# A hybrid encoder on one core: attention's first loads inside the projections, the short sequence's sums on DVE, and a group's last value products in front of its sums over keys

## Chip, core and metric

One core of one Trainium2 chip runs the whole layer. The metric is the device time in microseconds (us); three runs of the kernel before were timed, and one more execution was profiled. The engines are named as the profile names them: PE is TensorE (PEld its weight loads), DVE is VectorE, ACT is ScalarE, POOL is GpSimd, SP is SyncE, which issues nearly all transfers (SPq is its queue).

## The reference

One encoder layer on two requests that share weights: a prompt of 1024 tokens and a sample of 2048, 1024 channels, each with 256 memory tokens. All numbers are fp32.

```python
h = rms_norm(x, norm_pre)
z = einsum('btd,de->bte', h, w_in)          # 2304 columns
u_pool, g_pool, q, k, v, g_attn, q_x, g_x = split(z, SPLITS)
pool_out = multiscale_pool(u_pool, pool_w, pool_scale) * silu(g_pool)   # windows 2, 4, 8, 16
q, k = apply_rope(rms_norm(q)), apply_rope(rms_norm(k))                 # 8 heads, 2 key/value heads, 64 wide
attn_out = softmax(q k^T / 8) v * silu(g_attn)                          # every query sees every key
x_out = softmax(q_x k_m^T / 8) v_m * silu(g_x)                          # 4 heads, 256 memory tokens
mix = concatenate([pool_out, attn_out, x_out])                          # 1024 columns
return x + rms_norm(einsum('bte,ed->btd', mix, w_out), norm_post)
```

## The kernel before

Matrix products keep fp32 accuracy by splitting each operand in a high part (type fp32r) and a rest: three matmuls, hi·hi, lo·hi and hi·lo, stand for one. The kernel has two phases, each with its own pools of SBUF and PSUM, and the second phase's pools open when the first one's have closed.

**Projections** (lines 72 to 427). Four super-blocks run one after the other: the memory tokens, the prompt, and the two halves of the sample. A token super-block has 1024 tokens in two blocks of 512 and walks over six groups of 384 columns of w_in (`tok_groups`): queries (`group_n0`), memory queries and gates (`ct[2]`), keys, values and the last queries (`group_n1`), pooling input and its first gate (`ct[0]`), gates (`ct[1]`), and memory query and gates (`ct[3]`). In a transposed group every `product` makes a 128×512 tile in PSUM (`pz`, four buffers) with 24 matmuls, eight channel chunks of three. Results go to scratch in DRAM through SP's queue: `dq`, `dqx` (queries), `dk`, `dkm` (keys), `dv`, `dvm` (values), `dg` (gates, after Silu), `dp` (pooled channels). The pooling mixer (`pool_chunk`) adds shifted copies on POOL in the buffers `s2`, `s4`, `sm`, multiplies on PE (`pm`), scales on DVE into `s4` and stores that to `dp`; the next chunk writes `s4` again.

**Attention** (lines 430 to 878). Work is cut into pairs of query tiles (256 queries): eight of the sample, then four of the prompt. A pair has three groups, one for each of the two key/value heads and one for the memory (kinds 0, 1, 2). A group has 16 chunks of 128 keys in the sample, 8 in the prompt and 2 in the memory; one chunk of one group is a slot, 344 in all. A hand-written order holds for PE, ACT, DVE and POOL. In a slot stand:

- `weights(k, 0)` and `weights(k, 1)`: scores S of 128 keys by 512 queries on PE (L595; L599 for the memory), from KA and qa, and from KB and qb; then exp on ACT into P (L602), six buffers.
- `sums(k-1)`: z, the running sum of P over chunks (L613), 1024 columns, cut by `CUT = 512`: the first 512 on POOL, the others on DVE.
- one `largest`, a "look": two matmuls (L567) or four (L559) make 1024 scores N in PSUM (pool `psn`, two buffers), and DVE reduces them (L570) to a row maximum. A group's looks run LEAD = 4 slots and more before the group. The twenty looks that the first groups need come ahead of slot 0.
- `values`, in runs of four chunks: acc, P times V (L625).
- at a group's end `totals` (L633: z times ones, over the partitions, into a buffer of `psn`), `take` (acc times gate), `inverse` (rz, which is written to DRAM as `rows` and read back as `gz`, spread over partitions), and `mix_out`: o times gz on POOL (L661), the cast to the high part of mix on ACT and the rest on POOL (both L784).
- pieces of an earlier pair's output product (L726 to L728), eight of three matmuls for each half of a token tile, until slot HOLD = 16 or 26 of the next pair; then squares on ACT, y on DVE (L752), the residual xr + y on POOL (L755) and the store.

The queries' and keys' first loads (`load`), and V, gates, w_out and norm_post (`load_late`, `load_w_out`, `load_npost`) go through SP's queue. The last pair's output stays in PSUM (`both`) and its two tiles take turns on one buffer each of xr and y.

What places a group's last value products and its totals, with n the group's first slot and c its chunks:

```python
            for k in range(0, c, RUN):
                ks = list(range(k, min(k + RUN, c)))
                at(n + ks[-1] + 1 + END, g.values, ks)
            at(n + c + 1 + END, g.totals)
```

Of the kernel before, what the change touches and what calls it, by code (L numbers as in the profile page):

```python
# [15 lines left out]
D = 1024  # L16
# [7 lines left out]
def encoder(ctx, tc, I, O):  # L24
# [46 lines left out]

    with ExitStack() as p1:
# [3 lines left out]
        pst = p1.enter_context(tc.tile_pool(name="pst", bufs=2, space=PSUM))  # L76
# [15 lines left out]
        def hT_block(sb, blk):  # L92
# [4 lines left out]
            for i in range(4):  # L97
                x = two.tile([128, D], F32, name="x", tag="x", bufs=4)
                nc.sync.dma_start(out=x, in_=rows(sb, blk, i))
                if kind not in gains:  # L100
                    gains[kind] = one.tile([128, D], F32, name="gain", tag="gain")
                    src = I["mem_norm" if kind == "mem" else "norm_pre"]
                    nc.sync.dma_start(out=gains[kind], in_=src.broadcast_to([128, D]))
                junk = one.tile([128, D], mybir.dt.bfloat16, name="junk", tag="junk")
                ss = two.tile([128, 1], F32, name="ss", tag="ss")
                nc.scalar.activation(out=junk, in_=x, func=AF.Square, accum_out=ss)
                r = rsqrt(two, ss, 1, D, "rsx")
# [27 lines left out]
        def product(ps, terms):  # L135

            n = len(terms)
            for c, (sh, sl, mh, ml) in enumerate(terms):
                nc.tensor.matmul(ps, lhsT=sh, rhs=mh, start=c == 0, stop=False)  # L139
                nc.tensor.matmul(ps, lhsT=sh, rhs=ml, start=False, stop=False)  # L140
                nc.tensor.matmul(ps, lhsT=sl, rhs=mh, start=False, stop=c == n - 1)  # L141

# [9 lines left out]
        def transposed(hT, w, col):  # L152
# [3 lines left out]
            product(ps, [(w[0][:, c, f], w[1][:, c, f], hT[0][:, c], hT[1][:, c]) for c in range(NC)])  # L156
# [5 lines left out]
        def rope_tables():  # L162
            out = []
            raw = [two.tile([128, NTT, 64], F32, name="ropec", tag="ropec", bufs=1),
                   two.tile([128, NTT, 64], F32, name="ropes", tag="ropes", bufs=1)]
            for r, key in zip(raw, ("rope_c", "rope_s")):
                nc.sync.dma_start(out=r, in_=I[key])
            for key in ("k_norm", "q_norm"):
                g = one.tile([128, 2, 64], F32, name="hg", tag="hg" + key)
# [9 lines left out]
                for j in range(2):  # L179
                    if key == "q_norm":  # L180
                        t = raw[j]
                    else:
                        t = one.tile([128, NTT, 64], F32, name="ropek", tag=f"ropek{j}")
# [7 lines left out]
        def norm_rope(ps, parts, tt):  # L191
# [3 lines left out]
            z = two.tile([128, 384], F32, name="z", tag="z")  # L195
            sq = two.tile([128, 384], F32, name="sq", tag="sq")
            t1 = two.tile([128, 384], F32, name="t1", tag="t1")
            nc.scalar.copy(out=z[:, 0:w], in_=ps[:, 0:w])
            nc.scalar.activation(out=sq[:, 0:w], in_=ps[:, 0:w], func=AF.Square)
            ss = two.tile([128, 6], F32, name="ssh", tag="ssh")  # L200
# [3 lines left out]
            r = rsqrt(two, ss[:, 0:n], n, 64, f"rsh{n}")  # L204
# [22 lines left out]
        def heads_transposed(src, npair):  # L227
# [4 lines left out]
            o = two.tile([128, 2, 3, 128], F32R, name="qst", tag="qst")  # L232
# [20 lines left out]
        def group_n1(s, b, hT, w):  # L253
            for i in range(4):
                tt = 4 * b + i
                ps = natural(hT, w, i, 0, 384)
                vst = two.tile([128, 2, 64], F32, name="vst", tag="vst")
# [104 lines left out]
        def chunks_group(chunks):  # L362
            def run(s, b, hT, w):
                for k, (_, f, args) in enumerate(chunks):
                    f(s, b, *args, transposed(hT, w, 128 * k))
# [25 lines left out]
        def mem_v(s, b, hT, w):  # L391
            for i in range(4):
                ps = natural(hT, w, i, 0, 256).rearrange("p (h d) -> p h d", d=64)
                vst = two.tile([128, 4, 64], F32, name="vmst", tag="vmst", bufs=1)
# [15 lines left out]

        for sb, (kind, s, nb, b0) in enumerate(SB):
            groups = groups_of(sb)
            nxt = []
            for gi, (src, pieces, run) in enumerate(groups):
# [5 lines left out]
                final = gi + 1 == len(groups)  # L420
                for blk in range(nb):
                    if kind == "mem" and gi == 0 and blk == 0:
                        nxt.append(hT_block(sb + 1, 0))
                    run(s, b0 + blk, cur[blk], w)
# [5 lines left out]
    with ExitStack() as p2:  # L430
        def pool(name, bufs, space=bass.MemoryType.SB):
            return p2.enter_context(tc.tile_pool(name=name, bufs=bufs, space=space, reuse_waits="tile"))

        one = pool("p2one", 1)
        two = pool("p2two", 2)
        pss = pool("pss", 2, PSUM)
        psn = pool("psn", 2, PSUM)
        psa = pool("psa", 1, PSUM)
        pso = pool("pso", 1, PSUM)

        ones = one.tile([128, 32], F32, name="ones")
        nc.vector.memset(ones, 1.0)

        KA = [one.tile([128, 2048], F32R, name=f"KA{kind}") for kind in range(2)]
        KB = [one.tile([128, 2048], F32R, name=f"KB{kind}") for kind in range(2)]
        KA.append(one.tile([128, 2, 2, NMEM], F32R, name="KA2"))
        KB.append(one.tile([128, 2, 2, NMEM], F32R, name="KB2"))
        for t in KB:  # L450
            nc.vector.memset(t[64:65].bitcast(F32), 1.0)
        V = [one.tile([128, 16, 64], F32, name=f"V{kind}") for kind in range(2)]
        V.append(one.tile([128, 2, 4, 64], F32, name="V2"))
        has_K, has_V = set(), set()

        def load_K(s, kind):
            has_K.add((s, kind))
            for hl in range(2):
                for t, h in ((KA, 64 * hl), (KB, 0))[:2 - hl]:
                    if kind == 2:  # L460
                        src = DKM[hl, :, :, s].rearrange("d (c j) m -> d c j m", j=2)
                        nc.sync.dma_start(out=t[2][h:h + 64].bitcast(F32), in_=src)
                        continue
                    for a in range(0, SEQS[s][1], 1024):
                        nc.sync.dma_start(out=t[kind][h:h + 64, a:a + 1024].bitcast(F32),
                                          in_=DK[s][kind][hl, :, a:a + 1024])

        def load_V(s, kind):
            has_V.add((s, kind))
            if kind == 2:  # L470
                nc.sync.dma_start(out=V[2], in_=DVM[s])
                return
            for a in range(0, SEQS[s][1] // 128, 8):
                nc.sync.dma_start(out=V[kind][:, a:a + 8], in_=DV[s][kind][:, a:a + 8])

        wo_hi = one.tile([128, NC, D], F32R, name="wo_hi")
        wo_lo = one.tile([128, NC, D], F32R, name="wo_lo")
        raws = {}

        def load_w_out(c):  # L480
            raws[c] = two.tile([128, D], F32, name="raw", tag=("y", "xr")[c % 2], bufs=1)
            nc.sync.dma_start(out=raws[c], in_=I["w_out"][0, 128 * c:128 * c + 128])

        def split_w_out(c):
            raw = raws.pop(c)
            nc.scalar.copy(out=wo_hi[:, c], in_=raw)
            nc.gpsimd.tensor_tensor(out=wo_lo[:, c], in0=raw, in1=wo_hi[:, c].bitcast(F32), op=ALU.subtract)

        npost = one.tile([128, D], F32, name="npost")

        def load_npost():
            nc.sync.dma_start(out=npost, in_=I["norm_post"].broadcast_to([128, D]))


        lanes32 = {}
        for name in ("top",):
            lanes32[name] = [one.tile([128, 32], F32, name=f"{name}{n}") for n in range(2)]
            for t in lanes32[name]:
                nc.vector.memset(t, 0.0)

        def lanes_to_rows(t, name):

            r = two.tile([128, 32], F32, name="rows32", tag=f"r{name}")
            nc.vector.transpose(out=r, in_=t)
# [416 lines left out]
```

## Time and profile before

| | |
|---|---|
| runs | 1940.56, 1941.95, 1943.42 us; median 1941.95 |
| profiled execution | 1940.45 us; span from first to last instruction 1938.6 us |
| granted TensorE clock | 0.974 mean |
| busy | PE 1830.0 us (94%), DVE 1126.4 (58%), POOL 914.3 (47%), ACT 699.3 (36%) |
| projections end on PE | 691.78 us |
| first exp of attention | 747.73 us |
| first slots of the pairs 9 to 12 (prompt) | 1601.2, 1672.4, 1746.8, 1820.8 us |
| last matmul | 1923.7 us |

Times are microseconds from the first instruction. In a timeline row stand start, duration, engine, line, operation, output and inputs, and in brackets how long the engine had been idle and what ended that. The row of a tile gives minimum, median and maximum of its durations in nanoseconds.

### The profile page before, as it was taken

To read this page: it belongs to the slowest core of one execution; us is meant where nothing else is said; L and a number is where in the kernel's file an instruction comes from. 1 tells how busy PE (TensorE), PEld (TensorE's weight loads), DVE (VectorE), ACT (ScalarE), POOL (GpSimd) and SP (SyncE) were. 2 spreads that over 40 slices of the span, in tenths; PEclk is the share of its full clock that TensorE was granted. 3 is DMA by queue.
4 is the path that set the end of the run, shared out by engine and by line. 5 is a ranking of instruction groups with operands and counts; after the bars stand their busy time and mean duration, and the time that the engine had idled before them with its cause. 6 is when DMAs were issued, how large, how long until landed. Compare 5 with 4: busy or idle time off the path is not lost.

```text
span 1938.6 us, 23683 instructions
## 1 busy us (share of the span) xinstructions
PE 1830.0 (94%) x8520; PEld 1289.7 (67%) x8520; DVE 1126.4 (58%) x1304; ACT 699.3 (36%) x1266; POOL 914.3 (47%) x816
## 2 busy tenths in 40 slices
PE   7999999999999938999999999999999999999995
PEld 6998898978998824456565655656565655565564
DVE  6833254422623018876767677676767666756742
ACT  5522242313422102543434444443434443333331
POOL 3735033620634003863746456373746454635644
PEclk9999999999999967899999999999999999999998
DMA  6653355434443273212112021222212143323211
GB/s 235 200 147 89 110 161 138 116 100 123 118 123 86 66 176 118 82 39 77 60 47 80 26 79 44 77 60 77 61 48 78 49 125 83 93 77 104 82 39 60
DMA packets 148486, 181.84 MB, mean 94 GB/s; under 512 B 21504, under 2 KB 118416, under 8 KB 148368
## 3 DMA queue, kind: packets, MB, share of 16 engines
q1 hardware_dynamic: 148368, 180.33, 32.6%
q8 instruction: 67, 1.10, 0.2%
q14 instruction: 51, 0.42, 0.1%
HBM read 126.50 MB, written 53.62 MB: 93 GB/s over the span
## 4 chain that ended last, share of the span: by engine, by line
PE 70%; issue 10%; DVE 8%; POOL 6%; DMA 4%; ACT 2%; SPq 1%; POOLq 0%; ACTq 0%; DVEq 0%
PE acc L625 13%; PE S L595 11%; PE pz L141 9%; PE pz L139 9%; PE pz L140 9%; PE N L567 6%; PE py L726 3%; PE py L727 3%; PE py L728 3%; DVE nb L570 2%; POOL z L613 2%; DVE z L613 2%; PE S L599 1%; POOL rs L63 1%; PE N L633 1%
## 5 line engine op out<-in xcount | busy, mean ns | idle before, releaser
L602 ACT ACTIVATE P<-S 128x512 f32<-128x512 f32 x688 | 401.3, 599 | 612.8 <-PE S L595 435.4
L613 POOL TENSOR_TENSOR z<-z,P 128x512 f32<-128x512 f32 x272 | 389.2, 1431 | 260.3 <-ACT P L602 253.9
L570 DVE TENSOR_REDUCE nb<-N 128x1 f32<-128x1024 f32 x256 | 311.0, 1218 | 229.0 <-PE N L567 228.2
L625 PE MATMUL acc<-P,V 128*64 128x512 f32 (+1 forms) x1472 | 318.2, 574 | 0.5
L595 PE MATMUL S<-qa,KA 128*128 128x512 f32 x640 | 277.3, 433 | 11.6 <-ACT P L602 11.5
L613 DVE TENSOR_TENSOR z<-z,P 128x512 f32<-128x512 f32 x272 | 262.2, 964 | 15.9 <-ACT P L602 15.4
L567 PE MATMUL N<-KA,qa 128*128 128x512 f32 x640 | 217.0, 423 | 46.1 <-DMA qa<-dq 29.5
L595 PE MATMUL S<-qb,KB 65*128 65x512 f32 x640 | 255.2, 399 | 0.0
L139 PE MATMUL pz<-hT_hi,w_hi 128*128 128x512 f32 x592 | 233.2, 394 | 2.6 <-ACT w_hi L68 1.8
L140 PE MATMUL pz<-hT_lo,w_hi 128*128 128x512 f32 x592 | 233.9, 395 | 0.0
L141 PE MATMUL pz<-hT_hi,w_lo 128*128 128x512 f32 x592 | 232.3, 392 | 0.0
L595 PEld LDWEIGHTS S<-qa,KA 128*128 128x128 f32 x640 | 121.7, 190 | 146.4 <-issue 71.9
L625 PEld LDWEIGHTS acc<-P,V 128*64 128x64 f32 x1472 | 98.1, 137 | 177.6 <-issue 168.5
L567 PEld LDWEIGHTS N<-KA,qa 128*128 128x128 f32 x640 | 119.3, 198 | 97.5 <-DVE nb L570 35.1
L63 POOL TENSOR_TENSOR rs<-rs,mhalf 128x1 f32<-128x1 f32 (+2 forms) x100 | 92.9, 932 | 175.7 <-DVE rs L61 175.5
L570 DVE TENSOR_REDUCE top<-N 128x1 f32<-128x1024 f32 (+1 forms) x88 | 107.1, 1218 | 109.5 <-PE N L567 79.6
L613 POOL TENSOR_TENSOR z<-P 128x512 f32<-128x512 f32 x36 | 46.6, 1294 | 215.4 <-ACT P L602 154.3
L140 PE MATMUL pz<-w_lo,hT_hi 128*128 128x384 f32 (+1 forms) x416 | 140.5, 338 | 0.9 <-DVE w_lo L69 0.8
L141 PE MATMUL pz<-w_hi,hT_lo 128*128 128x384 f32 (+1 forms) x416 | 140.2, 338 | 0.0
L139 PE MATMUL pz<-w_hi,hT_hi 128*128 128x384 f32 (+1 forms) x416 | 139.4, 336 | 0.0
L726 PE MATMUL py<-wo_hi,mix 128*128 128x512 f32 x352 | 138.0, 392 | 0.0
L727 PE MATMUL py<-wo_lo,mix 128*128 128x512 f32 x352 | 137.2, 390 | 0.0
(115 smaller groups left out, 2587.5 us busy)
## 6 DMA issues: line engine op xcount, KB each, us to landing
wraw<-w_in SPq DMA_DIRECT2D x15, 1536.0 KB
dg<-gst SPq DMA_DIRECT2D x48, 256.0 KB
qa<-dq SPq DMA_DIRECT2D x48, 256.0 KB
gz<-rows SPq DMA_DIRECT2D x72, 128.0 KB
x<-x_sample SPq DMA_DIRECT2D x16, 512.0 KB
xr<-x_sample SPq DMA_DIRECT2D x16, 512.0 KB
y_sample<-xr SPq DMA_DIRECT2D x16, 512.0 KB
dq<-qst SPq DMA_DIRECT2D x48, 128.0 KB
```

Of the source, the lines that this page charges most:

```text
L63: nc.gpsimd.tensor_tensor(out=r, in0=r, in1=mhalf[:, 0:n], op=ALU.pow)
L139: nc.tensor.matmul(ps, lhsT=sh, rhs=mh, start=c == 0, stop=False)
L140: nc.tensor.matmul(ps, lhsT=sh, rhs=ml, start=False, stop=False)
L141: nc.tensor.matmul(ps, lhsT=sl, rhs=mh, start=False, stop=c == n - 1)
L567: nc.tensor.matmul(S[:, 512 * b:512 * b + 512], lhsT=q, rhs=KA[self.kind][:, k:k + 512], start=True, stop=True)
L570: nc.vector.tensor_reduce(out=out, in_=S, axis=AX.X, op=ALU.max, negate=True)
L595: nc.tensor.matmul(S, lhsT=K[self.kind][rows_, keys], rhs=q, start=n == 0, stop=n == 1)
L602: nc.scalar.activation(out=self.P[k][:, j], in_=S, func=AF.Exp)
L613: e.tensor_tensor(out=z[:, x], in0=a[:, x], in1=P[:, x], op=ALU.add)
L625: nc.tensor.matmul(self.acc[64 * j:64 * j + 64, x], lhsT=v, rhs=P[:, j, x], start=(k, i) == (0, 0), stop=k == self.chunks - 1, skip_group_ ...
L726: nc.tensor.matmul(ps, lhsT=mh, rhs=wo_hi[:, c, cols], start=first, stop=False)
L727: nc.tensor.matmul(ps, lhsT=mh, rhs=wo_lo[:, c, cols], start=False, stop=False)
```

## The change

The attention's definitions (`Group`, `Pair`, `Output`, the tables of slots and looks) now stand ahead of the projections, and their pools are renamed; that alone moves no instruction. Four things differ.

1. The projections' buffers that only the first three groups of a super-block need are in pools of their own (`front`) which close ahead of the last super-block's fourth group. In their place opens a pool `early` with KA, KB (without KB of kind 1), qa, qb and the looks' results, and the first groups' loads are issued there. The PSUM pool of the transposes (`heads`) closes ahead of the fifth group, and `psn` opens. In the sixth group PE's order is written out, and after every second channel chunk of a product stands one look. KB is loaded when a group's row maxima are turned into rows of qb (`shift`), KA before. KB of kind 1 lives in a pool that opens after the projections, and its row of ones is written there.
2. `CUT` is 0 for the prompt: its sums over keys are one DVE instruction of 1024 columns, and none on POOL.
3. A group's last run of values stands a slot later, directly in front of its totals.
4. The last pair's two output tiles take xr and y from the six buffers of P, and their loads are issued at their first piece.

```diff
+                if last and gi == 3:
+                    front.close()
+                    early = ctx.enter_context(tc.tile_pool(name="early", bufs=1, side="right", reuse_waits="tile"))
+                    open_early()
+                    for g in loads.pop(-1):
+                        g.load()
+                if last and gi == 4:
+                    heads.close()
+                    psn = ctx.enter_context(tc.tile_pool(name="psn", bufs=2, space=PSUM, side="right", reuse_waits="tile"))
...
+                    if last and final:
+                        with tc.manual_schedule(engines={mybir.EngineType.PE}):
+                            run(s, b0 + blk, cur[blk], w, look_ahead)
...
+        def product(ps, terms, beside=lambda: None):
...
                 nc.tensor.matmul(ps, lhsT=sl, rhs=mh, start=False, stop=c == n - 1)
+                if c % 2:
+                    beside()
...
+    def look_ahead():
+        if ahead:
+            g, n = ahead.pop(0)
+            g.largest(n)
...
-        with tc.manual_schedule(engines=order):
-            with tc.high_priority(offset=2000):
-                for g in loads.pop(-1):
-                    g.load()
-                for g, n in ahead:
-                    g.largest(n)
...
         def load(self):
-                if (s, kind) not in has_K:
-                    load_K(s, kind)
+            for hl in range(2):
+                load_K(s, kind, KA, hl, 64 * hl)
...
         def shift(self):
...
+            load_K(self.s, self.kind, KB, 0, 0)
             self.load_q(self.qb[0:64], 1)
...
-        CUT = 512
+    CUT = (0, 512)
...
-                for e, x in ((nc.gpsimd, slice(0, CUT)), (nc.vector, slice(CUT, 1024))):
-                    e.tensor_tensor(out=z[:, x], in0=a[:, x], in1=P[:, x], op=ALU.add)
+            cut = CUT[self.s]
+            if cut:
+                nc.gpsimd.tensor_tensor(out=z[:, :cut], in0=a[:, :cut], in1=P[:, :cut], op=ALU.add)
+            nc.vector.tensor_tensor(out=z[:, cut:], in0=a[:, cut:], in1=P[:, cut:], op=ALU.add)
...
-                at(n + ks[-1] + 1 + END, g.values, ks)
+            at(n + ks[-1] + (2 if ks[-1] == c - 1 else 1) + END, g.values, ks)
...
         def start(self):
-                self.xr = two.tile([128, D], F32, name="xr", tag="xr", bufs=1)
+            tag = dict(tag="P", bufs=6) if self.last else dict(tag="xr", bufs=1)
+            self.xr = dbl.tile([128, D], F32, name="xr", **tag)
...
         def piece(self, h, c, first, final):
             if self.last:
                 if self.both is None:
+                    self.start()
                     self.both = psn.tile([128, 1024], F32, name="N", tag="N")
```

PE at the end of the projections, before (pz is a product's tile, N a look's; KA_5966 and KA_5967 are kinds 0 and 1, KA_5970 the memory):

```order
L139 MATMUL pz<-hT_hi,w_hi 128x512
L140 MATMUL pz<-hT_lo,w_hi 128x512
L141 MATMUL pz<-hT_hi,w_lo 128x512
L567 MATMUL N<-KA_5966,qa 128x512 x28
L559 MATMUL N<-KA_5970,qa 128x256 x8
```

and now, inside a product of the sixth group (KA_5376 is kind 0):

```order
L551 MATMUL pz<-hT_hi,w_lo 128x512
L191 MATMUL N<-KA_5376,qa 128x512 x2
L549 MATMUL pz<-hT_hi,w_hi 128x512
L550 MATMUL pz<-hT_lo,w_hi 128x512
L551 MATMUL pz<-hT_hi,w_lo 128x512
```

The looks stood in one block behind the last product; now one stands after every six matmuls of the sixth group's first five products.

SP's queue behind the projections' key stores, before:

```order
L237 DMA dk_114<-qst 64x2x128
L338 DMA dp_112<-s_5394 128x512
L343 DMA dg_2_0_98<-gst 512x1x128
L338 DMA dp_112<-s_5433 128x512
L343 DMA dg_3_0_107<-gst 512x1x128
```

and now:

```order
L649 DMA dk_114<-qst 64x2x128
L99 DMA KA_5378<-dk_114 64x1024 x4
L161 DMA qa<-dq_0_1_76 64x1024 x2
L96 DMA KA_5379<-dkm 64x4x256 x2
L161 DMA qa<-dqx_0_79 64x1024 x2
L99 DMA KA_5376<-dk_114 64x1024 x4
L161 DMA qa<-dq_0_0_75 64x1024 x2
L750 DMA dp_112<-s_5437 128x512
L755 DMA dg_2_0_98<-gst 512x1x128
```

Sixteen loads of 256 KB stand between the last dk store and the first dp store of that super-block.

PE in the prompt where a group ends (py is an output piece), before:

```order
L727 MATMUL py<-wo_lo,mix 128x512
L728 MATMUL py<-wo_hi,mix 128x512
L633 MATMUL N<-z,ones 32x256 x4
L595 MATMUL S<-qa,KA_5967 128x512
L595 MATMUL S<-qb,KB_5969 128x512
```

and now:

```order
L358 MATMUL py<-wo_lo,mix 128x512
L359 MATMUL py<-wo_hi,mix 128x512
L252 MATMUL acc<-P,V_6121 64x512 x8
L260 MATMUL N<-z,ones 32x256 x4
L220 MATMUL S<-qa,KA_5378 128x512
L220 MATMUL S<-qb,KB_6119 128x512
```

The last eight value products, which stood a slot earlier, now stand directly in front of the totals.

More of the change, by code (lines that the diff above doesn't have):

```diff
@@ new lines, in encoder @@
+    looks, n = {}, len(slots)
+    left = {g: list(range(len(g.pieces))) for g in groups}
+    while any(left.values()):
+        n -= 1
+        able = [g for g in groups if left[g] and first[g] - LEAD > n]
+        if able:
+            looks[n] = (able[0], left[able[0]].pop())
+    ahead = [looks[n] for n in sorted(looks) if n < 0]
+    loads = {}
+    for n, (g, k) in looks.items():
+        if k == 0:
+            loads.setdefault(max(n - 3, -1), []).append(g)
+    order = {mybir.EngineType.PE, mybir.EngineType.Activation, mybir.EngineType.DVE,
+             mybir.EngineType.Pool}
@@ new lines, in pool @@
+    def pool(name, bufs, space=bass.MemoryType.SB):
+        return ctx.enter_context(tc.tile_pool(name=name, bufs=bufs, space=space, reuse_waits="tile"))
+    own = pool("p2one", 1)
+    dbl = pool("p2two", 2)
+    pss = pool("pss", 2, PSUM)
+    psa = pool("psa", 1, PSUM)
+    pso = pool("pso", 1, PSUM)
+    ones = own.tile([128, 32], F32, name="ones")
+    nc.vector.memset(ones, 1.0)
+    KB[1] = own.tile([128, 2048], F32R, name="KB1")
+    nc.vector.memset(KB[1][64:65].bitcast(F32), 1.0)
+    V += [own.tile([128, 16, 64], F32, name=f"V{kind}") for kind in range(2)]
@@ new lines, in encoder @@
+    V.append(own.tile([128, 2, 4, 64], F32, name="V2"))
+    wo_hi = own.tile([128, NC, D], F32R, name="wo_hi")
+    wo_lo = own.tile([128, NC, D], F32R, name="wo_lo")
+    npost = own.tile([128, D], F32, name="npost")
+    with tc.manual_schedule(engines=order):
+        slot = 0
+        while slot < len(slots) or later or fill:
+            g, k = slots[slot] if slot < len(slots) else (None, 0)
+            if g:
+                g.weights(k, 0)
+            if 0 < slot <= len(slots):
+                h, kh = slots[slot - 1]
+                h.sums(kh)
+            for x in loads.get(slot, ()):
+                x.load()
+            if slot in looks:
+                looks[slot][0].largest(looks[slot][1])
+            due(slot)
+            if g:
+                g.weights(k, 1)
+            pauses = sum(x is None for x in fill)
+            n = -(-(len(fill) - pauses) // max(1, until[0] - slot - pauses)) if fill else 0
+            for _ in range(n):
+                x = fill.pop(0)
+                if x is None:
+                    break
+                out, h, c, start, final = x
+                out.piece(h, c, start, final)
+                if final:
+                    if h == 0 and not out.last:
+                        for n in sorted(later):
+                            for x in [x for x in later[n] if x[0].__name__ in ("square", "norm", "out")]:
+                                later[n].remove(x)
+                                x[0](*x[1])
+                    at(slot + END, out.half_out, h)
+                    at(slot + 1 + END, out.square, h)
+                    if h == 1:
+                        at(slot + 2, out.norm)
+                        at(slot + 3, out.out)
+            due(slot + END)
+            slot += 1
```

711 lines of the change are left out of this document (327 added, 384 removed).

## The prediction

> **What bounds the kernel now.** I read the busy table first, then TensorE's (PE's) waits (engine, line, what was waited for: us in total, times, longest), the chain that ended last between 688 and 748 us, and the windows (us, PE busy, granted clock, DMA share, GB/s).
>
> ```profile
> PE 1830.0 (94%) x8520; PEld 1289.7 (67%) x8520; DVE 1126.4 (58%) x1304; ACT 699.3 (36%) x1266; POOL 914.3 (47%) x816
> ...
> PE N L567 <- DMA qa<-dq: 29.5, 1, 29.5
> PE N L633 <- POOL z L613: 16.9, 5, 6.6
> ```
> ```profile
> 691.54 0.24 PE pz L141
> 691.81 0.04 issue
> 691.86 0.61 ACT gst L342
> ...
> 695.66 6.12 DMA KA<-dk
> 701.80 9.65 DMA qa<-dqx
> 711.46 9.73 DMA qa<-dq
> 721.23 1.24 PE N L567 x2
> 722.49 1.24 DVE nb L570
> ...
> 746.92 0.77 PE S L599 x2
> ```
> ```profile
> 691.00:721.00 30.00, 0.77 (x4) 0.56 0.96 202
> 721.00:747.00 26.00, 23.77 (x47) 0.50 0.66 192
> 1756.00:1761.00 5.00, 5.00 (x26) 0.66 0.46 156
> ```
> ```profile
> 690.87 0.23 PE pz L141
> ...
> 692.47 1.28 ACT L602 ACT_TABLE_LOAD   x1
> 747.73 0.60 ACT L602 ACTIVATE P<-S 128x512 f32<-128x512 f32 x1 [53.97 <-PE S L599]
> ```
>
> PE bounds the whole with 1830 of 1938.6 us. The largest hole lies between the phases: PE ends the projections at 691.78 and gets its first look at 721.23, after the loads of KA and qa at 202 GB/s. The twenty looks then go at a clock of 0.50, PE and DVE in turn, 1.24 us each, to the first exp at 747.73. The second item is the wait of the sums over keys (L633) for POOL's half of z: 16.9 us in five times, of which 6.6 in the tail and 10.3 in the other four.
>
> **The change, part by part.** The sum is made against the profiled execution, 1940.45 us (span 1938.6); the median of the runs shown, 1941.95, stood 1.5 higher, and I add that at the end.
>
> *Loads and looks inside the projections.* From the last product's end (691.78) to the first exp (747.73) are 55.95 us. In their place PE gets 20 looks among warm products. A product's matmul of 512 columns takes .23 (690.87), so a look of two or four costs .46, together 9.2 us. One look follows six matmuls, so DVE has 6 × .23 + .46 = 1.84 us for a reduction of 1.24, and stays ahead. Between the last product and the first exp I leave 2.1 us: Silu .61, ACT's table load of 1.28, which now has nothing to hide behind, and the issue. The term is 11.3 − 55.95 = **−44.6**. Bounds: −46 if PE's next work covers the table load, −42 if a psn buffer is late a few times.
>
> These loads take a place on SP's queue. They stand directly behind the last dk stores and ahead of the pooling mixer's dp stores:
>
> ```profile
> 605.21 0.60 SPq L237 DMA_DIRECT2D dk<-qst  x1
> ...
> 608.74 1.06 POOL L304 TENSOR_TENSOR s<-s 128x525 f32<-128x525 f32 x1 [6.48 <-DMA dp<-s]
> ...
> 600.00:640.00 40.00, 40.00 (x174) 32.00 (x174) 10.44 (x13) 7.20 (x9) 12.78 (x13) 1.00 0.26 81
> ```
>
> Sixteen loads of 256 KB at about 205 GB/s are 20 us, from a DMA share of .26, so they land near 630, 30 us before the last group starts. But POOL's sums for the second pool chunk wait for the dp store ahead of them (608.74), so that chain comes nearly 20 us later, and its small product pm, which in the order now stands 54 matmuls (12 us) later, may wait: **+1.3**, between 0 (psz buffers cover it) and 3.
>
> *Start of attention.* What the pause hid comes back beside the first slots. The KB1 memset (1.76 below) stands on DVE between two looks. V2, gates, pg, pu, V0, two rows of w_out, KB1, V1, qa, qb and npost, 5.4 MB by the order's sizes, go to SP only when PE has let go of the projections' memory, and the first group's rows and gz stand behind them.
>
> ```profile
> 682.75 1.76 DVE L451 MEMSET KB<- 1x2048 f32 x1 [0.46 <-issue]
> ...
> 762.95 1.10 SPq L651 DMA_DIRECT2D gz<-rows  x2
> ...
> 772.09 1.76 POOL L661 TENSOR_TENSOR o<-o,gz 128x512 f32<-128x512 f32 x1
> ...
> 775.06 0.50 PE L595 MATMUL S<-qa,KA 128*128 128x512 f32 x1 [2.14 <-ACT P L602]
> ```
>
> 5.4 MB at 202 GB/s are 27 us, and rows and gz need some 4 us behind them: gz lands about 31 us after the first exp. POOL's product of o and gz stood 24.4 us after it (772.09 − 747.73). POOL runs in order and the cast behind it holds up ACT, whose exp PE waits for (775.06 shows the small form, 2.14). So I put +5 here, between 0 (the loads go faster, or three P buffers cover it) and +12 (V0 and KB1 late too), less 1 for the cold clock that the second group no longer meets: **+4**.
>
> *Last run of values in front of its totals, sample.* Before, PE had one slot's S and a look between them. The chain that follows totals (look, reduction, take, reciprocal, next look) keeps its length, and PE loses nothing there in the sample now: **0**, ±2.
>
> *Prompt: sums wholly on DVE, and values in front of the totals.*
>
> ```profile
> 1755.62 0.76 PE L633 MATMUL N<-z,ones 128*32 128x256 f32 x8 [3.23 <-POOL z L613]
> ...
> L613 DVE TENSOR_TENSOR z<-z,P x48: 627/938/1755, 1602.0 to 1889.9; 128x512 f32<-128x512 f32 x48
> ...
> L752 DVE SCALAR_TENSOR_TENSOR y<-y,rs,npost x22: 1275/1434/2285, 901.7 to 1891.0; 128x1024 f32<-128x1024 f32 x22
> ```
> ```profile
> 1741.00:1775.00 34.00, 29.83 (x132) 16.86 (x131) 27.74 (x29) 16.50 (x30) 29.55 (x20) 0.95 0.33 97
> 1741.00:1775.00 34.00, 0.76 (x8) 0.16 (x8) 10.03 (x10) 0.00 (x0) 14.88 (x10) 0.95 0.33 97
> 1672.00:1747.00 75.00, 70.99 (x324) 45.74 (x322) 47.15 (x49) 28.20 (x55) 40.18 (x29) 0.95 0.32 90
> ```
>
> The wait of 3.23 us comes once per pair, three times (10.3 − 3 × 3.23 leaves about .6 for the fourth), and the windows show a clock of .66 for 5 us behind it, so up to 5 × .34 = 1.7 more are lost; I take 1.5, 4.7 a time. The rows are the stretch 1741 to 1775, which has no output pieces, busy by engine (PE, PEld, DVE, ACT, POOL), then z's part of it. PE has 29.8 us of work there, 1.5 of it due to the clock, DVE 27.7, of which 10.03 are ten halves of z. After the change ten sums of 1024 columns stand on DVE. Nothing here shows that shape; the lower bound is two halves at their least, 1.25, and the nearest row is y, also 1024 columns from SBUF: 1.275 least, 1.434 median, 2.285 most. With POOL's z gone there is less to disturb DVE, so I take 1.29. DVE then needs 27.74 − 10.03 + 12.9 = 30.6 us of a stretch that PE would do in 28.3 + .7 of the usual waits. DVE becomes the bound, and with some 0.7 us it can't fill, the 34 us become about 31.3: −2.7, three times, and nothing in the first. **−8.** Bounds: −13 (PE bound everywhere) and +7 (1.8 us a sum: 35.7 us a stretch, four times +1.7).
>
> [...] POOL keeps o, mix and xr in these stretches.
>
> *Tail.*
>
> ```profile
> 1893.21 1.74 DVE L613 TENSOR_TENSOR z<-z,P 128x512 f32<-128x512 f32 x1
> ...
> 1896.04 2.33 POOL L755 TENSOR_TENSOR xr<-xr,y 128x1024 f32<-128x1024 f32 x1
> 1898.34 1.26 POOL L613 TENSOR_TENSOR z<-z,P 128x512 f32<-128x512 f32 x1
> 1899.65 1.08 PE L633 MATMUL N<-z,ones 128*32 128x256 f32 x8 [6.58 <-POOL z L613]
> ...
> 1928.24 1.41 DVE L752 SCALAR_TENSOR_TENSOR y<-N,rs,npost 128x512 f32<-128x512 f32 x2
> 1930.38 0.34 SPq L711 DMA_DIRECT2D xr<-x_prompt  x1
> 1933.66 0.69 DVE L755 TENSOR_TENSOR xr<-xr,y 128x512 f32<-128x512 f32 x1 [4.01 <-DMA xr<-x_prompt]
> 1933.70 1.77 POOL L755 TENSOR_TENSOR xr<-xr,y 128x512 f32<-128x512 f32 x1 [6.12 <-DMA xr<-x_prompt]
> ```
>
> The last totals waited 6.58 us for POOL, whose last half of z (1898.34) stood behind an xr of 2.33 us. DVE ended its own last half at 1894.95. Its sums become longer, but what stands ahead of them no longer contends with POOL's, so I let DVE end at about 1894.6 and PE go on there instead of 1899.65: **−5** (−3 to −6). At the very end the second tile's xr loads only after the first tile's stores have landed (1930.38), and its additions start at 1933.66. With buffers of their own they follow y: 1928.24 + 1.41, −.7 for the first half, so about 1928.9: 1933.66 − 1928.9 = **−4.8** (−4 to −5.5).
>
> Sum: −44.6 + 1.3 + 4 + 0 − 8 − 5 − 4.8 = **−57.1**, 1883.35 us for a profiled execution, 1885 as a median.
>
> **The rivals.**
> *The start of attention stalls.* If V0, KB1 and gz come late one after the other, the term is its upper bound, +11 instead of +4, and with more matmuls at the clock of .5 some 3 on top, 10 more than forecast: about 1895. For it: DMA at .96 busy at 202 GB/s in the pause. Against it: V is used only four slots after its chunk.
> *DVE eats the prompt gain.* If a sum costs 1.63 us, the stretch is 34 us again: term 0, 1893; at 1.8, 1900. For it: y's 2.285; against it: that value stood beside POOL's z.
> *DVE bounds the prompt so far that the kernel is slower.* A pair has DVE work of 47.15 us, some 16.6 of it in 15 halves, so 30.5 without. The other terms give 49; to lose these and 3.9 us more in four pairs, a pair of 75 us must become 88, so a sum must cost (88 − 30.5)/15 = 3.8 us. The row nearest in shape ends at 2.285.
> *It does not come early.* If the early loads wait for memory that the projections hold to their end, the first term falls away: −57.1 + 44.6 = −12.5, about 1929. Against it: the front pools close at the third group from the end, in the order the loads stand there.
>
> **How the numbers follow.** Forecast with its own bounds .55; the stall .21; DVE eating the gain .15; not early .05; slower .03; the rest is a run that lands within the measurement, .01. What a measurement of this kernel can tell from no change is about 0.2%, 3.9 us. The forecast's own range runs from 1875 (the prompt at −13 and the start at −1, 10 us better together) to 1890; with the stall and DVE's case it ends at 1902. Below I go to 1869, where tail, start and prompt all end at their better bounds. Faster .96, same .01, slower .03.
>
> **What would show it.** Looks standing between products from about 660 to 690 without a wait for a DMA; the first exp near 703 instead of 747.7; ACT's table load in front of it on the chain. POOL's product of o and gz waiting for gz between 727 and 735, and PE for ACT behind it. In the prompt no wait of L633's successor for POOL; z of 1024 columns at 1.25 to 1.45; PE's looks waiting for DVE instead, less than 1 us a slot. In the tail no xr load behind the first tile's stores. I am wrong if a sum costs over 1.6 us, or if PE's waits in the 35 us after the first exp exceed 15.

## The result, and the profile after

The changed kernel takes 1896.91 us (median of four runs, 1895.60 to 1903.27) against 1941.49 before; the ratio is 0.9776, with a 95% interval of 0.9752 to 0.9799. That is 44.6 us less. Forecast were 1885 us, 57 less, in a range of 1869 to 1902. The execution that was profiled is the fastest of the four, 1895.60 us.

From here on pairs are counted from 0: the prompt's are 8 to 11, which the table of the kernel before calls 9 to 12. The stages are told apart by the first exp of a group (L602 before, L227 after), read from the trace. The projections' end moves by up to 5 us between executions whose projections are the same: the first exp lies between 703.0 and 708.2 us in the profiles below. So kernels are compared from their first exp on, and the changed kernel's profile has the earliest one of all. Each kernel has one profile.

| stage, us | before | after | forecast | measured |
|---|---|---|---|---|
| to the first exp of attention | 747.7 | 703.0 | −43.3 | −44.7 |
| pair 0 | 94.7 | 95.5 | +4 | +0.8 |
| sample's pairs 1 to 7 | 758.7 | 757.1 | 0 | −1.7 |
| prompt, to the last group's first exp | 256.3 | 263.9 | −8 | **+7.6** |
| last group's first exp to the end | 81.1 | 74.3 | −9.8 | −6.9 |

Attention as a whole, from its first exp to the end, took 1190.9 us before and 1190.8 now: in these two profiles all of the gain is the pause. PE's waits after (engine, line, what was waited for: us in total, times, longest):

```profile
PE 1814.6 (96%) x8520; PEld 1281.5 (68%) x8520; DVE 1139.9 (60%) x1304; ACT 695.7 (37%) x1266; POOL 845.0 (45%) x756
...
PE S L220 <- ACT P L227: 25.1, 37, 6.1
...
PE pm L744 <- DVE sm L737: 2.7, 1, 2.7
...
PE N L260 <- POOL z L239: 1.6, 1, 1.6
PE N L260 <- DVE z L240: 1.4, 1, 1.4
```

The wait for qa's load (29.5) is gone, and of the 16.9 us that totals waited for POOL's z 1.6 are left. But PE waits 25.1 us for ACT's exp, where before it had waited 11.5:

```profile
PE S L595 <- ACT P L602: 11.5, 31, 2.1
```

The timeline at the phases' border shows the pause replaced as forecast, Silu, table load and exp one behind the other, 2.1 us behind the last product:

```profile
701.08 0.60 ACT L754 ACTIVATE gst<-pz 128x512 f32<-128x512 f32 x1 [5.32 <-PE pz L551]
701.70 1.28 ACT L227 ACT_TABLE_LOAD   x1
702.99 1.08 ACT L227 ACTIVATE P<-S 128x512 f32<-128x512 f32 x2
```

The rest of the story stands in 20 us of the prompt, where pair 8's last group ends (timeline of the changed kernel: start, us, engine, line, operation, and how long the engine was idle and what ended that):

```profile
1626.75 1.47 POOL L63 TENSOR_TENSOR rs<-rs,mhalf 128x1 f32<-128x1 f32 x1 [14.62 <-DVE rs L61]
...
1628.19 3.48 POOL L288 TENSOR_TENSOR o<-o,gz 128x512 f32<-128x512 f32 x2
...
1629.49 0.62 ACT L416 CAST mix<-o 128x512 fp32r<-128x512 f32 x1 [1.06 <-POOL o L288]
1630.47 2.28 DVE L240 TENSOR_TENSOR z<-z,P 128x1024 f32<-128x1024 f32 x1
1631.63 3.34 POOL L386 TENSOR_TENSOR xr<-xr,y 128x1024 f32<-128x1024 f32 x1
1631.70 0.62 ACT L416 CAST mix<-o 128x512 fp32r<-128x512 f32 x1 [1.58 <-POOL o L288]
1632.22 1.07 ACT L227 ACTIVATE P<-S 128x512 f32<-128x512 f32 x2
...
1632.87 0.79 PE L220 MATMUL S<-qa,KA 128*128 128x512 f32 x1 [3.14 <-ACT P L227]
...
1634.02 6.16 PE L252 MATMUL acc<-P,V 128*64 128x512 f32 x16
```

ACT's two casts of mix wait for POOL's two products o, and the exps that follow in ACT's order come after them. PE stands 3.14 us for these exps, and then its 16 value products take 6.16 us, at a granted clock of 0.56 from 1633 to 1640. Before, the same chain was there, at the same place:

```profile
1671.99 3.49 POOL L661 TENSOR_TENSOR o<-o,gz 128x512 f32<-128x512 f32 x2
...
1672.75 3.65 PE L625 MATMUL acc<-P,V 128*64 128x512 f32 x16
1673.31 0.62 ACT L784 CAST mix<-o 128x512 fp32r<-128x512 f32 x1 [0.27 <-POOL o L661]
...
1675.52 0.62 ACT L784 CAST mix<-o 128x512 fp32r<-128x512 f32 x1 [1.59 <-POOL o L661]
...
1676.05 0.59 ACT L602 ACTIVATE P<-S 128x512 f32<-128x512 f32 x1
```

but the 16 value products stood beside it, from 1672.75 to 1676.4, and hid it: PE's next S follows at 1676.33 without a wait. The change moved them a slot on, to hide the wait for z, and uncovered this one.

### The profile page after: what moved, and what is told of

Same layout as the page of the kernel before. It is cut to its first block, busy times and chain, and to the rows that moved or that the text cites. A ratio compares the mean times of both kernels' runs of the same rounds, so it can differ in the third digit from the quotient of the medians.

```text
span 1893.7 us, 23579 instructions
## 1 busy us (share of the span) xinstructions
PE 1814.6 (96%) x8520; PEld 1281.5 (68%) x8520; DVE 1139.9 (60%) x1304; ACT 695.7 (37%) x1266; POOL 845.0 (45%) x756
## 5 line engine op out<-in xcount | busy, mean ns | idle before, releaser
L227 ACT ACTIVATE P<-S 128x512 f32<-128x512 f32 x688 | 398.3, 598 | 561.8 <-PE S L220 480.5
L239 POOL TENSOR_TENSOR z<-z,P 128x512 f32<-128x512 f32 x224 | 319.1, 1425 | 243.8 <-ACT P L227 239.0
L252 PE MATMUL acc<-P,V 128*64 128x512 f32 (+1 forms) x1472 | 322.7, 581 | 0.0
L220 PE MATMUL S<-qa,KA 128*128 128x512 f32 x640 | 272.7, 426 | 25.2 <-ACT P L227 25.1
L240 DVE TENSOR_TENSOR z<-z,P 128x512 f32<-128x512 f32 (+1 forms) x272 | 276.9, 1018 | 20.2 <-ACT P L227 19.8
L191 PE MATMUL N<-KA,qa 128*128 128x512 f32 x640 | 208.1, 406 | 17.5 <-DVE rz L272 7.7
L191 PEld LDWEIGHTS N<-KA,qa 128*128 128x128 f32 x640 | 115.2, 190 | 64.5 <-DVE nb L194 26.9
L357 PE MATMUL py<-wo_hi,mix 128*128 128x512 f32 x352 | 137.7, 391 | 0.0
L359 PE MATMUL py<-wo_hi,mix 128*128 128x512 f32 x352 | 137.5, 391 | 0.0
```

The lines of the kernel that those rows point to most:

```text
L191: nc.tensor.matmul(S[:, 512 * b:512 * b + 512], lhsT=q, rhs=KA[self.kind][:, k:k + 512], start=True, stop=True)
L220: nc.tensor.matmul(S, lhsT=K[self.kind][rows_, keys], rhs=q, start=n == 0, stop=n == 1)
L227: nc.scalar.activation(out=self.P[k][:, j], in_=S, func=AF.Exp)
L239: nc.gpsimd.tensor_tensor(out=z[:, :cut], in0=a[:, :cut], in1=P[:, :cut], op=ALU.add)
L240: nc.vector.tensor_tensor(out=z[:, cut:], in0=a[:, cut:], in1=P[:, cut:], op=ALU.add)
L252: nc.tensor.matmul(self.acc[64 * j:64 * j + 64, x], lhsT=v, rhs=P[:, j, x], start=(k, i) == (0, 0), stop=k == self.chunks - 1, skip_group_ ...
```

## The experiments

**Taking parts 2 and 3 back, each alone and both.** In front of the totals (e1), in the sums' cut (e2), or both (e3):

```diff
 e1, e3
-            at(n + ks[-1] + (2 if ks[-1] == c - 1 else 1) + END, g.values, ks)
+            at(n + ks[-1] + 1 + END, g.values, ks)
 e2, e3
-    CUT = (0, 512)
+    CUT = (512, 512)
```

> The changed kernel with part 3 undone: a group's last values stand a slot earlier again, with S, a look and S between them and the totals; sums of the prompt wholly on DVE as changed. Theory A (in the prompt the values covered ACT's wait for POOL's products o, and moved away from there they leave PE waiting 3.1 us a pair): the 3.14 us waits of S for P in the prompt go, nothing waits for z at the totals, the four prompt pairs take 70 to 73 us instead of 72 to 77, and the time is 1881 to 1887. Theory B (DVE is the bound with whole sums, wherever the values stand): the pairs keep 75 to 77 us, 1894 to 1899. In the sample either theory expects less than 2 us.

> The changed kernel with part 2 undone: POOL takes half of each sum in the prompt again, values in front of the totals as changed. Theory A: the wait for ACT's P stays about 3 us a pair, POOL's z is covered by values and by that wait, pairs 74 to 77 us; the last totals wait for POOL some 5 us more: 1897 to 1903. Theory B: the prompt loses what DVE's whole sums cost and gains what the values cover, pairs 70 to 72 us, 1885 to 1892.

> Parts 2 and 3 both undone: only the early loads and looks, and the last pair's buffers, remain. Both theories: the prompt's pairs as before (74.4 us, a 3.2 us wait for POOL's z each), so 7 to 8 us better there than the changed kernel, and the last totals about 5 us later again: 1893 to 1897. If the early loads and looks, not parts 2 and 3, lengthened the prompt, it stays at 1900 or more.

| | time, us | first exp to end | pair 0 | prompt | tail |
|---|---|---|---|---|---|
| before | 1941.5 | 1190.9 | 94.7 | 256.3 | 81.1 |
| after (2 and 3) | 1896.9 | 1190.8 | 95.5 | 263.9 | 74.3 |
| e1 (2 without 3) | 1900.1 | 1191.3 | 98.6 | 258.6 | 74.8 |
| e2 (3 without 2) | 1897.4 | 1188.4 | 95.1 | 259.5 | 76.6 |
| e3 (neither) | 1900.2 | 1190.2 | 98.4 | 256.1 | 76.5 |

The ratios to before are 0.9788 (0.9769 to 0.9808) for e1, 0.9769 (0.9750 to 0.9788) for e2 and 0.9787 (0.9771 to 0.9802) for e3, so by their times these three and the changed kernel can't be told apart; the stages can. e3 says that the early loads leave the prompt as it was (−0.3), and that the buffers of part 4 are worth 4.7 us in the tail. On top of e3, part 2 alone costs the prompt 2.5 us, part 3 alone 3.4, and both together 7.9; the first two are hardly more than kernels with the same order of instructions differ by (below). e3's time lay above the 1893 to 1897 expected: its first exp came at 708.2, and its tail lost 2.2, not 5. e2 came as theory A has it: the wait for ACT is there with POOL's z as well,

```profile
PE S L220 <- ACT P L227: 22.2, 36, 5.9
PE N L260 <- POOL z L239: 7.8, 2, 6.6
```

2.4 us in each of three pairs, and the prompt is 3.2 longer than before, while theory B wanted it shorter. e1 hit neither: the waits for ACT went, and 5.4 of the 7.6 us with them, but instead of a gain PE waited for DVE, 2.0 us for the reciprocal rz (1646.63 to 1648.60 in pair 9) and .3 to .6 for reductions. Ahead of that reciprocal stands a wait of DVE's own, for POOL's rest of mix:

```profile
1646.20 0.69 DVE L266 TENSOR_TENSOR o<-acc,gate 128x512 f32<-128x512 f32 x1 [1.28 <-POOL mix L416]
...
1648.61 0.73 PE L191 MATMUL N<-KA,qa 128*128 128x512 f32 x2 [1.97 <-DVE rz L272]
```

So theory A holds, the values uncover ACT's wait. Of theory B a part holds: beneath that wait DVE is late, but it is busy for 21.5 of the 24.7 us of pair 9's first group and waits for POOL itself. Pair 0's column shows a gain of part 3 that I had put at nothing: 3 us, in the third group, where e1 waits 2.19 us for a look's reduction; in the pairs 1 to 7 it is another 2.3.

**Casts later.** ACT's casts of mix, and POOL's rests behind them, two slots later in the prompt (kind 1 excepted).

```diff
+        d = 2 if pair.s == 0 and c != BASE[1] else 0
-        at(slot + 1 + END, nc.scalar.copy, hi, a)
-        at(slot + 2, nc.gpsimd.tensor_tensor, lo, a, hi.bitcast(F32), ALU.subtract)
+        at(slot + 1 + d + END, nc.scalar.copy, hi, a)
+        at(slot + 2 + d, nc.gpsimd.tensor_tensor, lo, a, hi.bitcast(F32), ALU.subtract)
```

> The changed kernel, with ACT's casts of mix (pooled channels, heads of kind 0 and memory) and POOL's rests two slots later in the prompt's pairs, so that ACT does not reach them before POOL has made o. Theory A: the 3.14 us wait in three pairs goes with the cold clock behind it, the pairs take 71 to 74 us, 1882 to 1888. Theory B (DVE is the bound): no change, 1894 to 1899, with PE waiting for DVE where it waited for ACT.

1893.79 us, ratio 0.9756 (0.9739 to 0.9772); from the first exp 1183.4, 7.4 less than the changed kernel, the prompt 256.8.

```profile
PE S L220 <- ACT P L227: 14.7, 31, 5.9
```

The 3.14 us waits are gone, with the values where the change put them: the chain over POOL's o and ACT's casts is shown as their cause. The pairs 9 and 10 take 73.1 and 74.0, in the upper half of theory A's range, and little less than the 74.4 and 74.0 of before. The time missed theory A's 1882 to 1888 and stands at the edge of theory B's. What holds the pairs now is DVE, with POOL beside it. Busy times in the first group of pair 9 (us, busy PE, PEld, DVE, ACT, POOL), and DVE's and POOL's rows around it:

```profile
1630.80:1654.90 24.10, 21.90 (x95) 11.62 (x94) 23.18 (x21) 10.95 (x22) 14.14 (x9) 0.93 0.35 110
```
```profile
1630.01 1.22 DVE L240 TENSOR_TENSOR z<-z,P 128x1024 f32<-128x1024 f32 x1
1633.89 2.30 DVE L240 TENSOR_TENSOR z<-z,P 128x1024 f32<-128x1024 f32 x1
1638.38 2.36 DVE L240 TENSOR_TENSOR z<-P 128x1024 f32<-128x1024 f32 x1
...
1631.61 3.50 POOL L288 TENSOR_TENSOR o<-o,gz 128x512 f32<-128x512 f32 x2
1635.08 3.33 POOL L387 TENSOR_TENSOR xr<-xr,y 128x1024 f32<-128x1024 f32 x1
1638.37 1.29 POOL L417 TENSOR_TENSOR mix<-pu,mix 128x512 fp32r<-128x512 f32 x1
```

DVE is busy for 23.18 of 24.10 us here, for 23.18 of 25.0 in pair 10 and for 21.88 of 25.2 in pair 11: it comes near the bound and is not all of it. A sum of 1024 columns takes 1.22, and 2.30 and 2.36 in the two places where POOL's products and its addition, or its rests of mix, run beside it. In pair 11 the second place comes out the other way round:

```profile
1785.52 2.35 POOL L417 TENSOR_TENSOR mix<-pu,mix 128x512 fp32r<-128x512 f32 x1
1785.53 1.21 DVE L240 TENSOR_TENSOR z<-P 128x1024 f32<-128x1024 f32 x1
...
1789.16 0.69 DVE L266 TENSOR_TENSOR o<-acc,gate 128x512 f32<-128x512 f32 x1 [1.29 <-POOL mix L417]
...
1791.57 0.72 PE L191 MATMUL N<-KA,qa 128*128 128x512 f32 x2 [1.96 <-DVE rz L272]
```

Here the sum keeps its 1.21 us, POOL's rest takes 2.35 instead of 1.29, and DVE's next product and the reciprocal come late for it. In both pairs the two start .01 us apart, in the same order of instructions. PE pays either way: 1.75 us for a reduction behind the long sum in pair 9, 1.96 for the reciprocal in pair 11.

**POOL's addition left out.** On top of the later casts, the second output tile of the pairs 7 to 9 is stored as y, without the residual.

```diff
+                bare = self.x == 1 and self.pair in pairs[7:10]
-                (nc.vector if h else nc.gpsimd).tensor_tensor(out=x[:, c], in0=x[:, c], in1=y[:, c], op=ALU.add)
+                if not bare:
+                    (nc.vector if h else nc.gpsimd).tensor_tensor(...)
-                                  in_=x[:, c])
+                                  in_=(y if bare else x)[:, c])
```

> The kernel with the later casts, where in addition the second output tile of the pairs 7 to 9 is stored without its residual (POOL's addition xr + y of 1024 columns, which falls into the prompt's stretches, is left out). Theory C (DVE is the bound there since POOL's two-operand work stretches its sums to 2.3 us): the sum beside it returns to 1.2 to 1.3 us, the pairs 9 to 11 start 1 to 2 us earlier each, from the first exp to the end 1179 to 1181 us instead of 1183.4. Rival (the long sums have another cause): unchanged within 1 us.

1884.5 us, ratio 0.9726 (0.9702 to 0.9749); from the first exp 1176.5, 6.9 less than with the later casts alone and more than expected: 6.1 of it in the prompt, .8 in the tail. The prompt takes 250.7 us, 5.6 less than before the change. The second of the two long sums is short again: POOL's rests, which stood beside it, come earlier without the addition. The first, beside POOL's o, is not:

```profile
1628.20:1650.90 22.70, 20.48 (x96) 10.49 (x94) 21.97 (x21) 10.77 (x21) 10.94 (x8) 1.00 0.32 93
```
```profile
1631.38 2.29 DVE L240 TENSOR_TENSOR z<-z,P 128x1024 f32<-128x1024 f32 x1
...
1635.86 1.21 DVE L240 TENSOR_TENSOR z<-P 128x1024 f32<-128x1024 f32 x1
```

That is 1.15 us in each of the pairs 9 and 10; in pair 11 this sum was short already, and POOL's rest long. PE's longest wait in this stretch is 1.17 us instead of 1.75, and the clock 1.00 instead of .93. How the 6.1 us divide between the sums, the waits and the clock is not shown.

**A quarter of the sums on POOL.** `CUT = (256, 512)` on top of the later casts.

> The kernel with the later casts, where POOL takes 256 of the 1024 columns of the prompt's sums. If DVE's time is the bound: ten sums of 768 columns save some 3 us of DVE a stretch, the pairs take 71 to 72.5 us instead of 73 to 74, from the first exp to the end 1177 to 1181 us. If POOL's queue (o, o and xr ahead of z) is what holds the totals: PE waits for POOL's z again, 2 us or more in each stretch, and the time is 1184 to 1190 us.

1900.4 us, ratio 0.9795 (0.9777 to 0.9813); from the first exp 1188.4. The second alternative came true: the totals wait for POOL's z again, 3.05 us in three pairs and 5.76 in the tail.

```profile
PE N L260 <- POOL z L239: 16.3, 5, 5.8
```

The amount of the sum on POOL matters little: it stands behind o, o and xr in POOL's queue. From the start of the first o to the end of that z are 8.6 us in pair 9 here, with 256 columns (1629.99 to 1638.58), and 9.2 in the kernel before, with 512 (1671.99 to 1681.17).

**w_out later.** A one-element memset on each tile of w_out and on norm_post, six slots later, holds their loads back, so that less stands ahead of the first group's gz.

```diff
+        nc.vector.memset(raws[c][0:1, 0:1], 0.0)
         nc.sync.dma_start(out=raws[c], in_=I["w_out"][0, 128 * c:128 * c + 128])
...
-        at(4 + 3 * c, load_w_out, c)
-        at(7 + 3 * c, split_w_out, c)
+        at(10 + 3 * c, load_w_out, c)
+        at(13 + 3 * c, split_w_out, c)
```

> The changed kernel, with w_out's rows and norm_post held back (a one-element memset on each tile in DVE's order) so that 1.5 MB less stand ahead of the first group's rows and gz on SP's queue. Theory (the 6.1 us wait at 727 us is gz queued behind the bulk loads): gz lands 6 to 7 us earlier, the wait falls under 1 us, the second group of the first pair takes 44 to 46 us instead of 49.7, and the time from the first exp to the end 1185 to 1187 us instead of 1190.7. Rival (gz is late for SP's order or for the round trip of rows, not for the bytes): the wait stays over 4 us and the time within 1 us of the changed kernel's.

1898.89 us, ratio 0.9794 (0.9777 to 0.9810); from the first exp 1190.3, .5 less: the rival's time, though half of the theory's mechanism is there. In the changed kernel the wait at 727 us and its chain read

```profile
721.25 0.55 SPq L274 DMA_DIRECT2D rows<-rz  x1
727.22 1.10 SPq L278 DMA_DIRECT2D gz<-rows  x2
731.00 1.26 POOL L288 TENSOR_TENSOR o<-o,gz 128x512 f32<-128x512 f32 x1 [4.46 <-DMA gz<-rows]
732.29 0.62 ACT L416 CAST mix<-o 128x512 fp32r<-128x512 f32 x1 [7.43 <-POOL o L288]
...
733.46 0.80 PE L220 MATMUL S<-qa,KA 128*128 128x512 f32 x1 [6.12 <-ACT P L227]
```

and here PE waits 3.13 us, from 726.22. The second group became 2.9 shorter, not 4 to 6, and the third group and the next pair then took .6 and 1.5 us longer. That w_out's casts and rests, six slots later, are what costs there is likely and not shown.

**The tail's order.** On top of the later casts (not in the last pair), pair 10's second output tile three slots later.

```diff
-                            at(slot + 3, out.out)
+                            at(slot + (6 if out.pair is pairs[-2] and out.x == 1 else 3), out.out)
```

> The kernel with the later casts (not in the last pair), and the second output tile of pair 10 scaled and added three slots later, so that its y and xr stand behind the last sum over keys and behind the rests of mix. Theory: the last totals no longer wait 1.4 us for DVE's z, and the first output pieces no longer 2.1 us for POOL's rest of mix, nor run at the low clock behind it: the tail from the last group's first exp to the end takes 69 to 71 us instead of 74.4. Rival (the tail is set by POOL's products o themselves): 73.5 to 74.5.

1887.54 us, ratio 0.9733 (0.9715 to 0.9750); from the first exp 1176.3. The tail takes 68.7 us instead of 74.4. Of the waits of 1.4 us for DVE's z and 2.1 for POOL's rest of mix .3 are left, and the output pieces run at full clock (1.00 from 1857 to 1870). That the casts of the last pair stand at their old place again is not the reason: the changed kernel, where they do too, has a tail of 74.3.

**All of those outputs later, and the first o later.** First the second tiles of the pairs 7 to 10 eight slots after their last product; then, in a second kernel, besides that the first group's mix four slots later.

```diff
-                        at(slot + (6 if out.pair is pairs[-2] and out.x == 1 else 3), out.out)
+                        at(slot + (8 if out.pair in pairs[-5:-1] and out.x == 1 else 3), out.out)
 second kernel, besides:
-            wait = max(first[g] + g.chunks + 5, free)
+            wait = max(first[g] + g.chunks + 5, free) + (4 if g is groups[0] else 0)
```

> The kernel with the tail order, where the second output tile of the pairs 7 to 10 is scaled and added eight slots after its last product instead of three (nothing is left out). Theory C (POOL's o and xr and DVE's y crowd the slots of a group's last sum and totals; elsewhere they cost less): the prompt's kind-0 groups of pairs 9 to 11 take 22.5 to 24 us instead of 23.6 to 25.2, the time from the first exp to the end is 1171 to 1175 us instead of 1176.3. Rival (DVE's total work bounds the stretch, wherever y stands): within 1 us of 1176.3.

> The same, and the first group's product of o and gz, its cast on ACT and its rest four slots later. Theory (the 6 us wait near 728 us is the chain gz, POOL's o, ACT's cast, exp, in engines that run in order): the wait goes altogether with the low clock behind it, the second group of the first pair takes 42 to 45 us instead of 49.6, and the time falls by 5 to 7 us against the kernel without it, from the first exp 1165 to 1169 us. Rival (it is given back, as when w_out came later: the next wait, for w_out's rows or the third group's values, takes its place): less than 2 us.

1890.39 us, ratio 0.9735 (0.9718 to 0.9751), from the first exp 1180.5; and 1882.68 us, ratio 0.9695 (0.9678 to 0.9712), from the first exp 1178.0. In the first, the prompt became 3.4 us longer than with the tail order alone (258.7 against 255.3): worse than either case. The kind-0 groups of the pairs 9 to 11 take 25.1 us each instead of 25.2, 23.6 and 24.0. DVE is busy for 22.0 of these 25.1 in pair 9, less than with the later casts, so its amount of work alone does not set the stretch. The last pair's memory group takes 15.1 instead of 12.6, with PE waiting 2.8 us for an exp.

In the second, 1.8 us at 739.5 have taken the place of the 6 us near 728, and pair 0 takes 90.6 us instead of 95.4, 4.8 of the 5 to 7 expected. From the first exp to the end only 2.5 are left of that, because the prompt takes 3.1 us longer in three memory groups, from the same order of instructions. In part this is again POOL beside DVE: two sums, of 2.32 us (1575.7) and 2.04 (1720.4), are long in the second kernel alone, and behind the later one PE waits 1.69 us. The rest stays open. By the medians the second kernel is 7.7 us faster than the first; the one profile of each comes from an execution 1.5 below the first's median and 2.7 above the second's.

**The two that paid, together.** The tail order and the first group's mix four slots later.

> The kernel with the tail order (outputs of pairs 7 to 9 at their old place) and the first group's product of o and gz four slots later. If the two gains add, the second group of the first pair takes 44.4 us, the tail 68.7 us, and the time from the first exp to the end is 1171 to 1173 us, about 5 less than with the tail order alone; the time 1880 to 1884 us.

1881.22 us (median of five runs), ratio 0.9706 (0.9693 to 0.9720). That is 15.7 us less than the changed kernel's median, of which some 2 belong to the session, where the kernel before took 1939.25 us instead of 1941.49. From the first exp it takes 1171.6 us, as expected, with a tail of 68.7 and a pair 0 of 87.9, 7.3 less than with the tail order alone. Of that the prompt gives 2.0 back (257.3 against 255.3) and the sample's pairs .6, from the same order of instructions. The traces show two things that differ in the prompt. With the tail order, POOL's rest was slowed in the pairs 9 and 10 and DVE's sum in pair 11; here it is the other way round. And the granted clock fell to .50 four times in the prompt here, and twice there. What a kernel's one profile gives for the prompt is therefore uncertain by up to 3 us.

## Why the prediction was right, and where it was wrong

The time lay inside the range, 12 us above the forecast and above the 1890 to which its own bounds went. The range reached it by what was added for the two rivals, DVE's load in the prompt and the stalled start; the chain over ACT, the largest single loss, stood in neither, so that the range held is in part luck. The largest term was right: −44.6 forecast for the pause, −43.3 with the wait of pm; the first exp came 44.7 earlier in this profile, 39.5 to 44.1 in the others with the same projections and 42.0 in the mean of all twelve, always against the one profile of before. The looks stood between products, no look waited for a load, and the table load stood alone in front of the first exp. POOL's later chain cost a wait of pm of 2.7 us, at the upper end of 0 to 3. What the term left out is the clock: in nine of the twelve profiles it fell to .50 behind this wait for 3.4 us, which costs about 1.7 more; the changed kernel's profile is not among them.

The start of attention was right in place and mechanism: rows and gz behind the bulk loads, POOL's o, ACT's cast, PE. The second group lost 4.3 us, +5 forecast before the clock's −1, and PE waited 9.5 us in the 35 us after the first exp, less than the 15 that were to show the forecast wrong. That the sum for pair 0 is +.8 is part 3's doing, whose 0 for the sample should have been about −5: without part 3 (e1) pair 0 is 3.9 longer than before.

The step that failed is "Prompt": −8 forecast, +7.6 measured. Its price for the sum was good for most of them: 1.29 taken, 1.215 the median of the changed kernel's sums. But 12 of the prompt's 60 sums take 2.0 to 2.3, above the 1.6 that was to show the forecast wrong, and the mean is 1.4. What was left out is what the value products had hidden in their old place. I costed the wait that they were moved to, 3.23, and never asked what ACT and POOL did in the slot that they left: the rows of before show a chain from POOL's o at 1671.99 to the exp at 1676.05, which ends as the values end. With it uncovered the 3.23 was exchanged for 3.14, with the low clock behind it as before.

From forecast to measured are 15.6 us. The casts' two slots give 7.1 of them back and bring the prompt to 256.8, near the 256.3 of before. Leaving out POOL's addition gives 6.1 more, so most of the missing gain went into POOL and DVE slowing each other and what PE waits for behind that. Some 2.4 stay open. That is near what I had as a rival, DVE as the bound, but its price, a sum of 1.63 or 1.8 throughout, was wrong in kind: most sums take 1.22, and three of a pair's fifteen take 2.0 to 2.3. The row named for it, y's 2.285, had stood beside POOL's o (1890.94 to 1894.41), which the change kept, not beside z.

In the tail the totals came 5.7 us earlier, as forecast, but the term took PE's way on for free. The first pieces need the rest of mix, which POOL had behind xr (2.1 us, then a clock of .50 from 1859 to 1863): −2.2 remained of −5. The second tile's own buffers brought 4.7 of the 4.8 forecast.

## What to carry to other kernels

Work that is moved in front of a wait has been hiding something where it was: read, for the slot that it leaves, every engine's row that ends with it, before the wait that it goes to is counted as won. In an engine that takes its work in order, as ACT does in the rows above, a cast that waits for a slow producer holds up everything behind it: PE stood 3.14 us for that. Placing the casts two slots later was worth 7.4 us here; handing a quarter of the sums back to POOL cost 5.0. A part of a sum that is moved off an engine gains little if what remains there stands behind the same queue: 8.6 us to the end of POOL's z with 256 columns, 9.2 with 512. And compare kernels by stages only down to what the same order of instructions gives twice: up to 3 us in the prompt here.

## What the runs showed of the hardware

A DVE addition of 128×1024 fp32 with both operands in SBUF takes 1.22 us alone and up to 2.36 beside POOL's additions and products; or else DVE keeps its 1.21, and POOL's rest of 128×512 takes 2.35 instead of 1.29. Both 2.36 and 2.35 are nearly the sum of the two alone, 1.22 and 1.29: one is done at its own pace and the other loses about that time. POOL's xr of 128×1024 takes 2.4 at the median of the changed kernel and 3.34 beside one of DVE's long sums (1631.63); DVE's reduction of 1024 columns from PSUM took 1.21 in the same microseconds (1632.67). For the one that loses it is nearly a factor of two: 2.36 against 1.22 for the sum, 2.35 against 1.29 for the rest of mix.

The granted clock fell to 0.50 during or behind many of PE's waits: for 3.4 us behind 2.14 in the kernel before (776.3 to 779.8), for 6.8 at 3.14 in the changed kernel (1632.3 to 1639.1), for 10.2 at 6.12 (727.7 to 738.0). The length of the wait alone does not decide: in the changed kernel 2.71 us for pm were not followed by it (1.00 from 630 to 650), while 1.75 were with the later casts (below); and at the same place, 1.62 us were followed by it with w_out later (0.55 from 1564 to 1566), and 1.64 were not in the changed kernel (1.00 there). With a quarter of the sums on POOL, only one of the three waits of 3.05 was followed by it, that in pair 10. The windows of the kernel with later casts around a wait of 1.75 us (1640.19 to 1641.93), one us or two each (us, PE busy, granted clock, DMA share, GB/s):

```profile
1640.00:1642.00 2.00, 0.25 (x2) 1.00 0.63 213
1642.00:1643.00 1.00, 1.00 (x5) 0.67 0.87 292
1643.00:1644.00 1.00, 1.00 (x4) 0.50 0.73 270
1644.00:1645.00 1.00, 1.00 (x4) 0.50 0.82 252
1645.00:1646.00 1.00, 1.00 (x4) 0.62 0.13 38
```
